# First-token products of the DeltaNet scans over 128 rows with zero tiles, in place of 16 rows

## Chip, cores, metric

One core of a Trainium2 chip. The metric is device microseconds (us) of one execution of the whole kernel. Before the change three runs gave 1980.45, 1980.38 and 1978.99 us, median 1980.38 us. The profiled execution took 1978.97 us, with a span from first to last instruction of 1977.2 us.

## The reference

One layer of a hybrid encoder over 1024 tokens, with 16 meta tokens put in front (1040 in all), 1024 channels, float32 throughout. What bears on the change is the gated DeltaNet branch, with 8 heads of 128 by 128 state, scanned forward and backward:

```python
h = rmsnorm(h_res, norm1_w)                       # h_res = [16 meta tokens, 1024 tokens]
q, k, v, z, b, a, ... = split(h @ w_in)           # q, k, v: 8 heads x 128
q, k, v = silu(depthwise_conv_centred([q, k, v])) # width 5
q, k = l2norm(q) * 128 ** -0.5, l2norm(k)
# for each head and direction, chunk by chunk:
#   L = strict_lower(beta * (k k^T) * decay);  solve (I + L) [u, w] = [beta v, beta e^g k]
#   v_new = u - w S;  o = (q e^g) S + (q k^T * decay) v_new
#   S     = S * e^g_last + (k e^(g_last - g))^T v_new
o = (o_fwd + o_bwd)[meta padding dropped];  o = rmsnorm(o) * silu(z)
```

After the scans come the short-convolution branch, gates, the output projection, and a SwiGLU block of 2816 hidden channels.

## The kernel before

The kernel has one long first phase (up to about 925 us) and then the projections and the SwiGLU block. In the first phase the input projection runs unit by unit: for each unit of 128 output channels, `dense_steps` (L328) multiplies the weights with the 1040 tokens, 24 products for each of two or three stretches of 320 to 512 tokens, each in split single-pass float32 halves. Names: `hTh` and `al` are the high and low parts of the input, `wh` and `wl` those of the weights, `pm` is the bank that they fill. Between these products a planner in the kernel places the rest: it keeps estimated clocks for TensorE, VectorE, ScalarE and GpSimd (`T`, advanced by the calls `pe(...)`, `V(...)`, `A(...)`), and resumes generators whose due time has come. Each generator issues a few instructions and yields the time at which its next step is due. So the order is fixed when the program is built, and instructions are issued on each engine in that order (`manual_schedule`).

Four generators work on a head in turn: `g_decay` (decays, into `PQ`), `g_norm` (norms of q and k, the products k k^T and k q^T), `g_inv` (inversion of I + L in 32-row blocks, partly over DRAM with small DMAs) and `g_scan` (the state recurrence). Chunks have 128 tokens here; chunk index 8 stands for the first 16 (meta) tokens, `META = 16`, whose slots are handled apart, with tiles of 16 rows:

- `g_norm`, L562 and L563: the first 16 tokens of `kT` (channels by tokens) are turned with a TensorE transpose (in the profile the helper's line, L98) into `pt[:16]`, and the 16x16 product k k^T is made. Then four transposes of the next chunks follow (`tok(0)`). L567 copies the turned tokens into `kn[:16, 8]`, L572 the product into `Nm`.
- `g_inv`, L696 to L698: the inverse of the 16x16 block comes back by DMA from DRAM into `Pm`, a tile of 16x16.
- `g_scan`, L788 to L796: transposes of `vT` in three groups of three, the first of which begins with the 16 tokens; L795 scales each into `vS`, on ScalarE.
- `g_scan`, L803: `Pm` times `vS[:16, 8]`, a product with 16 rows of contraction and 16 output rows; L806 (VectorE) scales the 16 rows into `w`; L808: `kn[:16, 8]` times `w[:16]`, 16 rows of contraction and 128 output rows, gives the state `S0` (L811) with which the forward scan starts. L853 to L899 are the scan's loop over chunks, all its products 128 by 128.

In the profile a float32 product that is not split takes two passes, so a product of this kind counts as two MATMULs, and a transpose as one. A MATMUL row reads, for example, `16*128 16x128`: 16 rows and 128 columns of the array in use, and a moving operand of 16 partitions by 128 elements.

Of the kernel before, what the change touches and what calls it, by code (L numbers as in the profile page):

```python
# [8 lines left out]
F32 = mybir.dt.float32  # L9
F32R = mybir.dt.float32r  # L10
I32 = mybir.dt.int32
AF = mybir.ActivationFunctionType
# [4 lines left out]
P = 128  # L17
# [3 lines left out]
META = 16  # L21
# [27 lines left out]
def encoder_layer(ctx: ExitStack, tc: tile.TileContext, x, meta, norm1_w, w_in, w_ba,  # L49
                  dn_conv_w, A_log, dt_bias, dn_norm_w, sc_conv_w, w_bdn, w_bsc,  # L50
                  w_out, norm2_w, w_gu, w_down, final_w, out):
    nc = tc.nc
# [12 lines left out]
    def uid(s):  # L65
        cnt["n"] += 1
        return f"{s}_{cnt['n']}"
# [7 lines left out]
    def psd():  # L75
        return ps.tile([P, 512], F32, tag="e", name=uid("pe"), bufs=3)

    def pss():
        return ps.tile([P, 512], F32, tag="d", name=uid("pd"), bufs=3)
# [15 lines left out]
    mm = nc.tensor.matmul  # L95

    def transpose(dst, src, n=P):
        nc.tensor.transpose(dst, src, ident[:n, :n])  # L98
# [18 lines left out]
    def wload(src, j):  # L117
        wh, wl, raw = staged([P, KT, P])
        nc.sync.dma_start(raw, src[j])
        split(wh, wl, raw)  # L120
        return wh, wl
# [136 lines left out]
    def pe(ns):  # L258
        T["pe"] += ns
        return T["pe"] + HOP  # L260

    def V(n, kind=0):
        return on("dve", (68 + 1.042 * n, 130 + 1.042 * n, 130 + 0.52 * n)[kind])

    def A(n):
        return on("act", 144 + 0.834 * n)
# [19 lines left out]
    def enqueue(lane, gen):  # L286
        j = Job(gen)
        if not lanes[lane]:
            spent[lane] = max(spent[lane], min(spent.values()))
        lanes[lane].append(j)  # L290
        return j
# [179 lines left out]
    def cs(c):  # L471
        return slice(META + c * P, META + (c + 1) * P)
# [32 lines left out]
    def norm_job(st_, ssk1, cc, ce, he, y, tmp, sk):  # L505
        nc.vector.tensor_tensor(out=ce, in0=cc, in1=he, op=ALU.mult)
        V(18)
        yield T["dve"] + DEP
        yield from rsqrt_steps(y, ssk1, tmp)
        nc.vector.tensor_tensor(out=sk, in0=y, in1=ssk1, op=ALU.mult)  # L510
        V(9)
# [25 lines left out]
    def g_norm(h, st_):  # L537

        kq = st_["kq"]
        kT, qT = kq[:, 0], kq[:, 1]  # L540
        small = dn.tile([P, 9, 12], F32, tag="small", name=uid("small"), bufs=3)
        st_["small"] = small
        ssk, ssq, rk2, ssk1, y, tmp, sk = (small[:, :, i] for i in range(7))
        cc, ce = small[:, :, 7:9], small[:, :, 9:11]
        nc.gpsimd.memset(small, 1.0)
        kn = dn.tile([P, 9, P], F32, tag="kn", name=uid("kn"), bufs=2)
        st_["kn"] = kn

        def square(src, dst, p=P):
            jk = dn.tile([P, P], F32, tag="jk", name=uid("jk"))  # L550
            nc.scalar.activation(jk[:p], src, AF.Square, accum_out=dst)
            return on("act", 400)
# [6 lines left out]
            return pt, pe(4 * 107)  # L559

        pt = psd()
        transpose(pt[:META, :P], kT[:, 0:META])  # L562
        mm(pt[:META, P:P + META], kT[:, 0:META], kT[:, 0:META], start=True, stop=True)  # L563
        t = pe(120)
        nxt = tok(0)
        yield t
        nc.scalar.copy(kn[:META, 8], pt[:META, :P])  # L567
        A(P)
        square(pt[:META, :P], ssk[:META, 8:9], META)
        Nm = dn.tile([META, META], F32, tag="Nm", name=uid("Nm"), bufs=2)  # L570
# [5 lines left out]
        for c2 in range(4):  # L576
            pt, t = nxt
# [5 lines left out]
            for c in range(2):  # L583
                for a, s in ((0, ssk), (1, ssq)):
                    t = square(pt[:, c, a], s[:, 2 * c2 + c:2 * c2 + c + 1])
# [31 lines left out]
        for c in range(NC):  # L617
# [3 lines left out]
            pk, t = nxt.pop(0)  # L621
# [15 lines left out]
                ask()  # L637
        enqueue("norm", norm_job(st_, ssk1, cc, ce, he, y, tmp, sk))

    def g_inv(h, st_):  # L640

        NP, Nm = st_["NP"], st_["Nm"]

        nd = dr.tile([4, NC, 2, 32, 32], F32, tag="nd", name=uid("nd"), bufs=2)
        ndm = dr.tile([META, META], F32, tag="ndm", name=uid("ndm"), bufs=2)
        fN = dn.tile([P, 32, 32], F32, tag="fN", name=uid("fN"))
# [42 lines left out]
        pdm = dr.tile([META, META], F32, tag="pdm", name=uid("pdm"), bufs=2)  # L691
        nc.sync.dma_start(pdm.unsqueeze(0), mP)
        yield T["dve"] + LAND
        for b in range(4):
            nc.sync.dma_start(NP[B(b), :, :, B(b)].rearrange("j c d i -> j (c d) i"), pd[b].rearrange("c d j i -> j (c d) i"))
        Pm = dn.tile([META, META], F32, tag="Pm", name=uid("Pm"), bufs=2)  # L696
        st_["Pm"] = Pm
        nc.sync.dma_start(Pm, pdm)  # L698

        Xe = dn.tile([P, NC, 32], F32, tag="Xe", name=uid("Xe"))  # L700
        XT = dn.tile([P, 2, 512], F32, tag="XT", name=uid("XT"))
# [21 lines left out]
        pt = pss()[:, :256].rearrange("p (c i) -> p c i", c=NC)  # L723
# [31 lines left out]
        pt = pss().rearrange("p (c i) -> p c i", c=NC)  # L755
# [16 lines left out]
    def g_scan(h, st_):  # L772
        nonlocal freed
        kq, vT, small, kn, NP, PQ, Pm = (st_[k] for k in ("kq", "vT", "small", "kn", "NP", "PQ", "Pm"))
        kT, qT = kq[:, 0], kq[:, 1]
        ssk, ssq, rk2, ssk1, y, tmp, sk = (small[:, :, i] for i in range(7))
        cc, ce = small[:, :, 7:9], small[:, :, 9:11]
        sso = small[:, :, 11]
        vS = dn.tile([P, 9, P], F32, tag="vS", name=uid("vS"))
        yield from take("scan")  # L780

        def newbank():
            return pss().rearrange("p (a n) -> p a n", a=4)

        for grp in ((8, 0, 7), (1, 2, 3), (4, 5, 6)):
            pt = newbank()
            for i, c in enumerate(grp):
                if c == 8:  # L788
                    transpose(pt[:META, i], vT[:, 0:META])
                else:  # L790
                    transpose(pt[:, i], vT[:, cs(c)])
            yield pe(330)
            for i, c in enumerate(grp):
                p = META if c == 8 else P
                nc.scalar.activation(vS[:p, c], pt[:p, i], AF.Copy, scale=sk[:p, c:c + 1])  # L795
                A(P)  # L796
        yield T["act"] + HOP

# [1 line left out]


        bank = newbank()
        mm(bank[:META, 0], Pm, vS[:META, 8], start=True, stop=True)  # L803
        yield pe(215)
        w = dn.tile([P, P], F32, tag="w0", name=uid("w"))
        nc.vector.tensor_scalar(out=w[:META], in0=bank[:META, 0], scalar1=ce[:META, 8, 0:1], scalar2=None, op0=ALU.mult)  # L806
        yield V(P, 1)
        mm(bank[:, 1], kn[:META, 8], w[:META], start=True, stop=True)  # L808
        yield pe(215)
        S0 = dn.tile([P, P], F32, tag="S0", name=uid("S"), bufs=2)  # L810
        nc.vector.tensor_copy(S0, bank[:, 1])  # L811
# [35 lines left out]
        for i in range(NC):  # L847
# [6 lines left out]
            t = pe(215 * len(act_))  # L854
# [5 lines left out]
            for d in act_:  # L860
                c = cd[d]
# [3 lines left out]
                t = V(P, 1)  # L865
# [5 lines left out]
            w = [None, None]  # L871
            v2 = [None, None]
            for d in range(2):
                c = cd[d]
                w[d] = dn.tile([P, P], F32, tag=f"w{d}", name=uid("w"))
                nc.scalar.activation(w[d], b2[:, 2 + d], AF.Copy, scale=ce[:, c, d:d + 1])  # L876
                t = A(P)
            for d in range(2):
                c = cd[d]
# [3 lines left out]
            if i < NC - 1:  # L883
# [3 lines left out]
                t = pe(430)  # L887
# [4 lines left out]
            if i < NC - 1:  # L892
                yield t
                for d in range(2):
# [6 lines left out]
                    t = V(P, 1)  # L901
# [30 lines left out]
        for c4 in range(2):  # L932
            oT = vS[:, 4 * c4:4 * c4 + 4]
            pt = newbank()
# [48 lines left out]
    def start_streams():  # L983
        nonlocal ndec, nnorm, ninv, nscan
        h = ndec
        if h < H and h < freed + 2 and not decs:
            decs.append([g_decay(h, heads[h]), T["dve"] + HOP, h])
            ndec += 1
        h = nnorm
        if h < H and h < ndec and h < freed + 2 and not norms and all(k in heads[h] and heads[h][k]() for k in ("tk", "tq")):  # L990
            norms.append([g_norm(h, heads[h]), T["dve"] + HOP, h])
            nnorm += 1
        h = ninv
        if h < H and not invs and heads[h].get("normed"):
            invs.append([g_inv(h, heads[h]), T["dve"] + HOP, h])
            ninv += 1
        h = nscan
        if h < H and not scans and heads[h].get("inverted") and "tv" in heads[h] and heads[h]["tv"]():
            scans.append([g_scan(h, heads[h]), T["dve"] + HOP, h])
            nscan += 1  # L1000
# [22 lines left out]
    with tc.tile_pool(name="st", bufs=1) as st:  # L1023
# [37 lines left out]
        scale = {}  # L1061
# [306 lines left out]
    dn = ph1.enter_context(tc.tile_pool(name="dn", bufs=1))  # L1368
# [299 lines left out]
    for j in range(KT):  # L1668
        w = wload(w_bsc, j)
# [12 lines left out]
    for j in range(KT):  # L1682
        w = wload(w_bdn, j)
# [114 lines left out]
    t = KT - 1  # L1798
# [40 lines left out]
    AA, bank, bank2, po2 = [A0, A1, None, None], [pss()], [None] * 4, [psd()]  # L1839
# [304 lines left out]
```

## Time and profile before

| what | value |
|---|---|
| three runs | 1980.45, 1980.38, 1978.99 us; median 1980.38 us |
| profiled execution | 1978.97 us |
| its span | 1977.2 us, granted TensorE clock 0.999 |
| VectorE busy | 1395.8 us (71%), 3017 instructions |
| ScalarE busy | 838.5 us (42%) |
| GpSimd busy | 106.6 us (5%) |
| DMA | 251.52 MB, mean 127 GB/s |

PE is TensorE, PEld its weight loads, DVE is VectorE, ACT ScalarE, POOL GpSimd, SP the engine that issues most DMAs. Starts in the timeline are counted from the span's start. The end of a MATMUL is modelled, so this document reads TensorE's pace from the starts of successive MATMULs: what a group of instructions costs is the distance between starts around it, less the usual distance of the projection's products beside it.

### The profile page before, as it was taken

What the parts mean: (1) busy time and instruction counts of PE and PEld (TensorE: products, weight loads), DVE (VectorE), ACT (ScalarE), POOL (GpSimd) and SP (SyncE); (2) the same over time, 40 slices, a digit from 0 to 9 for tenths busy, and PEclk for the clock granted to TensorE, in tenths of its full rate; (3) what the DMA queues carried; (4) which work ended last, traced back from release to release, by engine and by line L of the source; (5) the groups of instructions that cost most, each with busy time, mean ns of one, the idle gap of its engine ahead of it and who ended that gap; (6) DMA issues with size and microseconds to landing.
All of it is one profiled execution on the core that took longest, in us unless ns stands there. A gap on an engine that the chain in (4) does not pass through costs nothing.

```text
span 1977.2 us, 31834 instructions
## 1 busy us (share of the span) xinstructions
PE 1961.2 (99%) x11992; PEld 1715.3 (87%) x11992; DVE 1395.8 (71%) x3017; ACT 838.5 (42%) x1968; POOL 106.6 (5%) x407
## 2 busy tenths in 40 slices
PE   9999999999999999999999999999999999999998
PEld 8999999999999999888888888888888888888887
DVE  7888688888888888844954544469676766746575
ACT  6472354636464646344444221225333333334344
POOL 2011101010101010100000000000000000000000
PEclk9999999999999999999999999999999999999999
DMA  4122122222222212222236752123366654477654
GB/s 145 59 88 81 55 87 60 76 60 76 60 76 60 76 60 76 70 87 90 102 128 229 252 167 97 65 86 111 124 220 243 253 183 165 170 278 243 193 176 165
DMA packets 124703, 251.52 MB, mean 127 GB/s; under 512 B 44988, under 2 KB 46453, under 8 KB 122117
## 3 DMA queue, kind: packets, MB, share of 16 engines
q1 hardware_dynamic: 123957, 248.44, 37.7%
q8 instruction: 94, 1.54, 0.3%
q10 hardware_dynamic: 592, 1.05, 0.1%
q14 instruction: 60, 0.49, 0.1%
HBM read 181.20 MB, written 68.25 MB: 126 GB/s over the span
## 4 chain that ended last, share of the span: by engine, by line
PE 92%; DVE 3%; DMA 2%; ACT 1%; issue 1%; SPq 0%; POOL 0%; DVEq 0%; POOLq 0%; ACTq 0%
PE pm L328 30%; PE pd L1441 14%; PE pe L1441 7%; PE pm L1441 5%; PE pe L136 2%; PE pe L135 2%; PE pe L134 2%; PE pd L869 1%; PE pd L890 1%; PE pd L853 1%; PE pe L2051 1%; PE pe L2052 1%; PE pe L2050 1%; PE pd L856 1%; PE pe L590 1%; PE pd L886 1%
## 5 line engine op out<-in xcount | busy, mean ns | idle before, releaser
L328 PE MATMUL pm<-hTh,wh 128*128 128x320 f32 (+4 forms) x1248 | 428.3, 348 | 0.3 <-ACT hTh L1091 0.2
L328 PE MATMUL pm<-al,wh 128*128 128x320 f32 (+4 forms) x1248 | 427.4, 348 | 0.0
L328 PE MATMUL pm<-hTh,wl 128*128 128x320 f32 (+4 forms) x1248 | 425.8, 346 | 0.1
L328 PEld LDWEIGHTS pm<-hTh,wh 128*128 128x128 f32 x1248 | 233.8, 188 | 12.8 <-issue 2.1
L328 PEld LDWEIGHTS pm<-hTh,wl 128*128 128x128 f32 x1248 | 233.9, 188 | 10.6 <-issue 0.4
L328 PEld LDWEIGHTS pm<-al,wh 128*128 128x128 f32 x1248 | 233.9, 188 | 9.7
L102 DVE TENSOR_TENSOR al<-raw,ring_h 128x1024 fp32r<-128x1024 f32 x73 | 88.6, 1222 | 64.7 <-ACT ring_h L101 63.9
L101 ACT CAST ring_h<-raw 128x1024 fp32r<-128x1024 f32 x73 | 76.6, 1053 | 106.2 <-PE pe L2052 35.0
L350 DVE SCALAR_TENSOR_TENSOR kq<-ra,wc,kq 128x520 f32<-128x520 f32 x128 | 96.5, 754 | 4.7 <-ACT kq L380 3.4
L977 DVE TENSOR_TENSOR wl<-raw,wh 128x512 fp32r<-128x512 f32 x112 | 75.8, 687 | 31.4 <-ACT wh L980 30.9
L876 ACT ACTIVATE w<-pd,small 128x128 f32<-128x128 f32 x128 | 39.8, 363 | 125.2 <-PE pd L869 124.6
L483 DVE TENSOR_TENSOR tm<-fP,fN 128x135 f32<-128x135 f32 (+23 forms) x248 | 71.6, 289 | 5.4 <-POOL mP L682 1.0
L487 DVE TENSOR_TENSOR fP<-fP,tm 128x135 f32<-128x135 f32 (+23 forms) x248 | 71.4, 288 | 5.1
L980 ACT CAST wh<-raw 128x512 fp32r<-128x512 f32 x112 | 66.3, 621 | 3.7 <-issue 3.6
L101 ACT CAST wh<-raw 128x1024 fp32r<-128x1024 f32 x37 | 38.8, 1048 | 46.6 <-PE pm L135 14.8
L1989 ACT ACTIVATE b<-b 128x512 f32<-128x512 f32 x20 | 12.6, 631 | 104.5 <-DVE b L1407 104.5
L843 ACT ACTIVATE jk<-NP 128x128 f32<-128x128 f32 x64 | 19.9, 311 | 76.5 <-DVE NP L839 75.4
L1441 PE MATMUL pd<-b_hl,wh 128*128 128x512 f32 x168 | 51.9, 390 | 0.0
L899 DVE SCALAR_TENSOR_TENSOR S<-S,eGl,pd 128x128 f32<-128x128 f32 x104 | 31.5, 340 | 28.0 <-PE pd L886 27.9
L863 DVE SCALAR_TENSOR_TENSOR r<-pd,negEG,vS 128x128 f32<-128x128 f32 x120 | 36.7, 344 | 20.4 <-PE pd L853 20.2
L1407 DVE TENSOR_TENSOR b<-pd,b 128x512 f32<-128x512 f32 x21 | 14.5, 689 | 51.8 <-PE pd L1441 51.8
L102 DVE TENSOR_TENSOR wl<-raw,wh 128x1024 fp32r<-128x1024 f32 x37 | 45.1, 1218 | 7.4 <-ACT wh L101 7.3
(629 smaller groups left out, 4783.0 us busy)
## 6 DMA issues: line engine op xcount, KB each, us to landing
raw<-in_w_in_dram SPq DMA_DIRECT2D x72, 512.0 KB
raw<-in_w_gate_up_dram SPq DMA_DIRECT2D x44, 512.0 KB
sums<-in_w_down_dram SPq DMA_DIRECT2D x22, 512.0 KB
t_d<-sums SPq DMA_DIRECT2D x11, 1024.0 KB
raw<-s_d SPq DMA_DIRECT2D x44, 256.0 KB
raw<-t_d SPq DMA_DIRECT2D x44, 256.0 KB
act_d<-b SPq DMA_DIRECT2D x43, 256.0 KB
raw<-act_d SPq DMA_DIRECT2D x33, 256.0 KB
```

The costliest lines, as they stand in the source:

```text
L101: nc.scalar.copy(hi, src)
L102: nc.vector.tensor_tensor(out=lo, in0=src, in1=hi.bitcast(F32), op=ALU.subtract)
L134: mm(po[:m, :n], wh[:, k, :m], xhk[:, t0:t0 + n], start=(k == 0), stop=False)
L135: mm(po[:m, :n], wh[:, k, :m], xlk[:, t0:t0 + n], start=False, stop=False)
L328: mm(po[:, :n], ww[:, k], f(k)[:, t0:t0 + n], start=i == 0, stop=i == 3 * KT - 1)
L350: nc.vector.scalar_tensor_tensor(out=acc, in0=raw[:, h0 + t:h0 + t + hn], scalar=wc[:, t, col:col + 1], in1=acc, op0=ALU.mult, op1=ALU.add)
L483: nc.vector.tensor_tensor(out=tv, in0=fP[:, 0:r, j:j + 1].broadcast_to([P, r, n]), in1=fN[:, j:j + 1, j + 1:32].broadcast_to([P, r, n]), o ...
L487: nc.vector.tensor_tensor(out=fP[:, 0:r, j + 1:32], in0=fP[:, 0:r, j + 1:32], in1=tv, op=ALU.subtract)
L876: nc.scalar.activation(w[d], b2[:, 2 + d], AF.Copy, scale=ce[:, c, d:d + 1])
L977: nc.vector.tensor_tensor(out=u[1][1][:, k], in0=u[2][:, k], in1=u[1][0][:, k].bitcast(F32), op=ALU.subtract)
L980: nc.scalar.copy(u[1][0][:, k], u[2][:, k])
L1441: mm(po, x[:, k], at(y, k), start=i == 0 and not add_to, stop=i == 11, skip_group_check=add_to)
```

## The change

All products and copies of the first 16 tokens are made over 128 rows and columns. In `g_norm` the first 128 tokens of `kT` are turned, and their whole 128x128 product is made; of it the 16x16 corner is used as before. `kn[:, 8]` gets 128 rows, of which 16 matter. Three tiles of 128x128, `wide`, are made once and set to zero on GpSimd in `g_inv` of the first head. Two of them take the place of `Pm`, for even and odd heads: the DMA fills the 16x16 corner alone. The third takes the place of `w`: VectorE writes its first 16 rows. In `g_scan` the first 128 tokens of `vT` are turned and scaled, and the two products (L803 and L808 before, L801 and L806 after) contract over 128 rows; zeros stand against whatever is in rows 16 to 127.

```diff
         pt = psd()
-        transpose(pt[:META, :P], kT[:, 0:META])
-        mm(pt[:META, P:P + META], kT[:, 0:META], kT[:, 0:META], start=True, stop=True)
+        transpose(pt[:, :P], kT[:, 0:P])
+        mm(pt[:, P:2 * P], kT[:, 0:P], kT[:, 0:P], start=True, stop=True)
...
-        nc.scalar.copy(kn[:META, 8], pt[:META, :P])
+        nc.scalar.copy(kn[:, 8], pt[:, :P])
...
-        Pm = dn.tile([META, META], F32, tag="Pm", name=uid("Pm"), bufs=2)
-        st_["Pm"] = Pm
-        nc.sync.dma_start(Pm, pdm)
+        if not wide:
+            wide.extend(dn.tile([P, P], F32, tag=f"wide{i}", name=uid("wide")) for i in range(3))
+            for t in wide:
+                nc.gpsimd.memset(t, 0.0)
+        Pm = st_["Pm"] = wide[h % 2]
+        nc.sync.dma_start(Pm[:META, :META], pdm)
...
-                if c == 8:
-                    transpose(pt[:META, i], vT[:, 0:META])
-                else:
-                    transpose(pt[:, i], vT[:, cs(c)])
+                transpose(pt[:, i], vT[:, 0:P] if c == 8 else vT[:, cs(c)])
             yield pe(330)
             for i, c in enumerate(grp):
-                p = META if c == 8 else P
-                nc.scalar.activation(vS[:p, c], pt[:p, i], AF.Copy, scale=sk[:p, c:c + 1])
+                nc.scalar.activation(vS[:, c], pt[:, i], AF.Copy, scale=sk[:, c:c + 1])
...
-        mm(bank[:META, 0], Pm, vS[:META, 8], start=True, stop=True)
+        mm(bank[:, 0], Pm, vS[:, 8], start=True, stop=True)
         yield pe(215)
-        w = dn.tile([P, P], F32, tag="w0", name=uid("w"))
+        w = wide[2]
         nc.vector.tensor_scalar(out=w[:META], in0=bank[:META, 0], scalar1=ce[:META, 8, 0:1], scalar2=None, op0=ALU.mult)
         yield V(P, 1)
-        mm(bank[:, 1], kn[:META, 8], w[:META], start=True, stop=True)
+        mm(bank[:, 1], kn[:, 8], w, start=True, stop=True)
```

The planner's estimates are the same numbers in both kernels, and so is the order on every engine, but for three instructions on POOL. TensorE around the first head's two products, with the size of the result at a row's end (L803 has 16 rows of it), before:

```order
L328 MATMUL pm<-hTh,wh 128x384
L328 MATMUL pm<-al,wh 128x384
L803 MATMUL pd<-vS,Pm 16x128
L328 MATMUL pm<-hTh,wl 128x384
L328 MATMUL pm<-hTh,wh 128x384
L328 MATMUL pm<-al,wh 128x384
L328 MATMUL pm<-hTh,wl 128x384
L328 MATMUL pm<-hTh,wh 128x384
L328 MATMUL pm<-al,wh 128x384
L808 MATMUL pd<-w,kn 128x128
L328 MATMUL pm<-hTh,wl 128x384
```

and after, where the same two products are L801 and L806:

```order
L328 MATMUL pm<-hTh,wh 128x384
L328 MATMUL pm<-al,wh 128x384
L801 MATMUL pd<-vS,wide 128x128
L328 MATMUL pm<-hTh,wl 128x384
L328 MATMUL pm<-hTh,wh 128x384
L328 MATMUL pm<-al,wh 128x384
L328 MATMUL pm<-hTh,wl 128x384
L328 MATMUL pm<-hTh,wh 128x384
L328 MATMUL pm<-al,wh 128x384
L806 MATMUL pd<-wide,kn 128x128
L328 MATMUL pm<-hTh,wl 128x384
```

Nothing moved; the six projection products between the two stay six. POOL in the first head's `g_inv`, after (`mP` is the 16x16 inverse, `ra` a row buffer of the convolutions, `XT` a tile of the inversion):

```order
L681 TENSOR_TENSOR mP<-mP,tm 1x15
L417 MEMSET ra 128x2
L698 MEMSET wide 128x128
L698 MEMSET wide 128x128
L698 MEMSET wide 128x128
L705 MEMSET XT 32x8x32
L706 MEMSET XT 32x8x32
L417 MEMSET ra 128x2
```

The three rows on `wide` are new, between `ra` and `XT`; the first head's DMA into `wide` waits for POOL, where that into `Pm` did not. The later heads' DMAs wait for what they waited for.

More of the change, by code (lines that the diff above doesn't have):

```diff
@@ L638, in g_norm @@
         enqueue("norm", norm_job(st_, ssk1, cc, ce, he, y, tmp, sk))
+    wide = []
     def g_inv(h, st_):
```

## The prediction

> **What bounds the kernel now.** I read the page first: how busy each engine is, and who stands on the chain of waits that ended last.
>
> ```profile
> PE 1961.2 (99%) x11992; PEld 1715.3 (87%) x11992; DVE 1395.8 (71%) x3017; ACT 838.5 (42%) x1968; POOL 106.6 (5%) x407
> PE 92%; DVE 3%; DMA 2%; ACT 1%; issue 1%; SPq 0%; POOL 0%; DVEq 0%; POOLq 0%; ACTq 0%
> ```
>
> TensorE is busy 99% of the span and holds 92% of the chain. So time that TensorE loses inside its own stream is time of the kernel, unless it falls where the chain lies on another engine. A busy share of 99% does not say that no pace is lost, since ends of MATMULs are modelled. So next I read the timeline of TensorE around the instructions that the change touches, by starts. The first head, around L803 and L808 (start, length, instruction; L328 is the projection):
>
> ```profile
> 214.40 0.34 PE L328 MATMUL pm<-al,wh 128*128 128x384 f32 x1
> 214.67 0.39 PE L803 MATMUL pd<-vS,Pm 16*16 16x128 f32 x2
> ...
> 215.27 0.34 PE L328 MATMUL pm<-hTh,wh 128*128 128x384 f32 x1
> 215.44 0.34 PE L328 MATMUL pm<-al,wh 128*128 128x384 f32 x1
> 215.62 0.33 PE L328 MATMUL pm<-hTh,wl 128*128 128x384 f32 x1
> ...
> 215.97 0.34 PE L328 MATMUL pm<-al,wh 128*128 128x384 f32 x1
> 216.23 0.48 PE L808 MATMUL pd<-w,kn 16*128 16x128 f32 x2
> ...
> 216.93 0.34 PE L328 MATMUL pm<-hTh,wh 128*128 128x384 f32 x1
> ```
>
> Undisturbed, an L328 product of 384 elements starts 0.17 to 0.18 us after the last one (215.27, 215.44, 215.62); call it 0.174. From 214.40 to 215.27 two such products and the two passes of L803 fit in: 0.87 - 2 x 0.174 = **0.52 us** for L803. From 215.97 to 216.93 the same way: 0.96 - 0.35 = **0.61 us** for L808. The last head, beside products of 512 elements:
>
> ```profile
> 875.94 0.40 PE L328 MATMUL pm<-hTh,wl 128*128 128x512 f32 x1
> ...
> 876.92 0.39 PE L328 MATMUL pm<-al,wh 128*128 128x512 f32 x1
> 877.15 0.39 PE L328 MATMUL pm<-hTh,wl 128*128 128x512 f32 x1
> 877.38 0.40 PE L328 MATMUL pm<-hTh,wh 128*128 128x512 f32 x1
> ...
> 878.46 0.40 PE L328 MATMUL pm<-hTh,wl 128*128 128x512 f32 x1
> ```
>
> Here the distance is 0.23; L803 costs 0.98 - 0.46 = 0.52 and L808 1.08 - 0.46 = 0.62. These are the first and the last of 8 heads. What do whole 128x128 products cost in the same place? The first head's next block, two products of two passes each:
>
> ```profile
> 217.62 0.34 PE L328 MATMUL pm<-al,wh 128*128 128x384 f32 x1
> 217.80 0.38 PE L853 MATMUL pd<-S,kq 128*128 128x128 f32 x2
> 218.02 0.39 PE L856 MATMUL pd<-S,kq 128*128 128x128 f32 x2
> ...
> 218.42 0.33 PE L328 MATMUL pm<-hTh,wh 128*128 128x384 f32 x1
> ```
>
> 0.80 - 0.35 = 0.45 us, so **0.226 us** for one product, 0.113 a pass. A product with an eighth of the rows costs more than twice as much as a whole one, on both sides of it: L803 starts 0.27 after the product before it instead of 0.17, and the product after it loses about as much. L853 has a semaphore to wait for as well and loses nothing, so I put the loss down to the change of shape in the array.
>
> [...]
>
> **The change part by part.** L803 becomes a whole product: 0.52 - 0.226 = 0.294 us, by 8 heads **2.35 us** gained. L808: 0.615 - 0.226 = 0.39, by 8 heads **3.1 us**. Next the first 16 tokens in `g_norm`, first and last head:
>
> ```profile
> 99.08 0.34 PE L328 MATMUL pm<-al,wh 128*128 128x384 f32 x1
> 99.26 0.27 PE L98 MATMUL pe<-ident,kq 128*16 128x128 f32 x1
> 99.46 0.21 PE L563 MATMUL pe<-kq 128*16 128x16 f32 x2
> ...
> 100.28 0.33 PE L328 MATMUL pm<-hTh,wh 128*128 128x384 f32 x1
> ```
>
> ```profile
> 764.75 0.34 PE L328 MATMUL pm<-al,wh 128*128 128x384 f32 x1
> ...
> 765.94 0.31 PE L328 MATMUL pm<-hTh,wh 128*128 128x322 f32 x1
> ```
>
> One narrow transpose, two narrow passes and four whole transposes cost 1.20 - 0.35 = 0.85, and 1.19 - 0.35 = 0.84. Afterwards they are seven whole passes, at 0.113 each 0.79. That gains 0.06 a head. The narrow passes lose their gap but get longer, and the two nearly cancel. Of the 8 places two, at 262.9 and 372.4 us, fall in stretches where the chain is not on TensorE (below) and count nothing: 6 x 0.06 = **0.36 us**. Bounds: nothing, if a pass costs 0.01 more than those of L853, and 0.28 a head, 1.7 us, if the two passes of the product hid wholly beside five transposes (0.57). The transposes of `vT`, one narrow and two whole:
>
> ```profile
> 301.16 0.34 PE L328 MATMUL pm<-hTh,wh 128*128 128x384 f32 x1
> 301.34 0.49 PE L98 MATMUL pd<-ident,vT 128*16 128x128 f32 x3
> ...
> 301.84 0.34 PE L328 MATMUL pm<-hTh,wl 128*128 128x384 f32 x1
> ```
>
> 0.68 - 0.35 = 0.33 for three, 0.11 each. They run at a whole pass's price already, and nothing is gained or lost: **0**.
>
> Off TensorE: ScalarE's copies (L567, L795) keep their elements per row, with more rows. GpSimd gets three fills, and the first head's DMA waits for them:
>
> ```profile
> L1246 POOL MEMSET Eb<- 128x128 f32 x1 | 0.2, 205 | 0.0
> 162.24 0.10 POOL L417 MEMSET ra<- 128x2 f32 x1 [6.43 <-DVE small L495]
> 194.91 0.48 SPq L698 DMA_DIRECT2D Pm<-pdm x1
> ```
>
> A fill of this size took 205 ns, three take 0.6 us. They stand ahead of 6.43 us in which POOL idled, over 30 us before the DMA is issued. So they cost **0**. Without that cover it would be 0.6 us, once.
>
> One wait remains for L803: the last of ScalarE's copies into `vS`.
>
> ```profile
> PEld pd L803 <- ACT vS L795: 2.2, 6, 0.4
> ```
>
> Its weight load idled 2.2 us in 6 heads, and the wait's last signal was ScalarE's. I take most of that as the gap itself, because L803 costs the same 0.52 in the first and in the last head while the copies end at other distances. But where the gap goes, ScalarE may be late by a part of it. Bounds are 0 and the whole of L803's gain, 2.35; I take 0.2 us, nearer to 0 since the gap after L803 cannot come from a wait before it.
>
> Sum: 2.35 + 3.1 + 0.36 - 0.2 = **5.6 us**. The profiled execution took 1978.97 us, and 1978.97 - 5.6 = 1973.4. It is at the low end of what was shown: with it and the three runs the mean is 1979.7. So I predict 1979.7 - 5.6 = **1974.1 us**, 0.28% faster.
>
> **The rivals.** First, the gain is made but waits take it back. The chain leaves TensorE for long in three places; entry and return of the first two, and the end of the third:
>
> ```profile
> 258.25 0.46 PE pd L853 x4
> 295.56 0.67 PE pe L590 x2
> 334.87 0.46 PE pd L869 x4
> 390.71 0.42 PE pd L736 x7
> 695.09 0.61 ACT XT L760
> ```
>
> All sixteen products L803 and L808 lie outside these stretches. If the other engines entered each stretch no earlier than now, TensorE would only wait longer, and what was gained before 695 us would be lost: heads 0 to 4, with L803 and L808 of heads 5 to 7 left, 3 x 0.68 + 0.1, **2.2 us**, hence 1977.5. For it speaks that DVE has little idle time there, a fifth in the row below. Against it: each stretch starts from a TensorE instruction, which moves earlier, and DVE has slack to follow.
>
> ```profile
> 218.00:258.70 40.70, 40.70 (x279) 38.64 (x278) 32.24 (x105) 14.42 (x49) 8.50 (x33) 1.00 0.14 42
> ```
>
> From the first head's L808 to the first stretch DVE was busy 32.24 of 40.70 us (the third number pair); 8.5 us of slack stands against 0.7 to make up.
>
> Second, on the other side: the gaps are no matter of shape, and stay. Then only the added work shows.
>
> ```profile
> L803 PEld LDWEIGHTS pd<-vS,Pm x16: 87/89/92, 214.7 to 876.3; 16*16 16x16 f32 x16
> L853 PEld LDWEIGHTS pd<-S,kq x240: 186/189/193, 217.6 to 919.0; 128*128 128x128 f32 x120
> ```
>
> A weight load of 16 columns took 89 ns, one of 128 columns 189: 0.1 us more for each of 16 passes of L803 and 16 of L563, 3.2 us. L563's 16 passes also stream 128 elements in place of 16, at most a whole pass's 0.113 each, 1.8 us. It decides if the loads cannot slip under the products before them while the gaps stay: **5.0 us slower**, 1984.7. Against it: whole products of L853 in the same stream hide all but 0.113 a pass.
>
> [...]
>
> Third, the change does only half of what it says: the gap before a product goes but the one after stays, as when it comes from the unsplit two-pass form. Then half, 2.8 us, 1976.9. Against it: L853 has two passes of this form, with no gap on either side.
>
> **How the numbers follow.** Forecast 0.78; waits take the gain back 0.10; half 0.06; gaps stay 0.04; anything else, such as TensorE's own pauses falling elsewhere, 0.02 on the slow side. The forecast's own bounds: 4.3 us of gain, with nothing from `g_norm` and half of L803's lost to its wait, to 7.1, with 1.7 from `g_norm` and no wait. With the runs' spread of 0.7 us to either side that is 1971.9 to 1976.1. The range reaches to the first rival: 1972.0 to 1977.5. A difference of 0.2%, 4 us, is about what a measurement of this kernel can tell from none. So faster 0.78, same 0.16, slower 0.06.
>
> **What would show it.** In the changed profile, starts around L801 and L806 should leave 0.23 us each; if 0.5 stays, the shape was not the reason. The `g_norm` block should cost 0.79, the `vT` group 0.33. The three stretches off TensorE should be as long as now, each entered earlier by what was gained before it; if they end at the same times, the first rival holds. Weight loads of L801 should not idle for `vS`. The part after 925 us should keep its length. The prediction is wrong if TensorE's waits for DVE and ACT grow by over 2 us in the first phase.

## The result, and the profile after

| what | before | after |
|---|---|---|
| median (14 runs each, same chip) | 1979.68 us (1978.12 to 1981.19) | 1975.4 us (1972.61 to 1978.34) |
| profiled execution, its span | 1978.97, 1977.2 us | 1978.34, 1976.6 us |

The ratio is 0.9979, interval 0.9971 to 0.9987: the change makes the kernel 4.3 us faster. Two repeats (below) gave 0.9973 and 0.9976. The profiled execution of after is the longest of its 14 runs, so its span hides most of the gain. The page of after, busy times and chain:

```profile
PE 1958.5 (99%) x11992; PEld 1721.5 (87%) x11992; DVE 1396.1 (71%) x3017; ACT 838.7 (42%) x1968; POOL 107.9 (5%) x410
PE 90%; DVE 4%; DMA 3%; ACT 1%; issue 1%; SPq 0%; DVEq 0%; ACTq 0%
```

TensorE has as many instructions as before and is 2.7 us less busy. That is all these two lines can say; the places of the change say more. TensorE's timeline of after around the first head's two products (start, length, instruction):

```profile
215.56 0.34 PE L328 MATMUL pm<-al,wh 128*128 128x384 f32 x1
215.74 0.38 PE L801 MATMUL pd<-vS,wide 128*128 128x128 f32 x2
215.88 0.42 PE L328 MATMUL pm<-hTh,wl 128*128 128x384 f32 x1
216.14 0.34 PE L328 MATMUL pm<-hTh,wh 128*128 128x384 f32 x1
...
216.83 0.34 PE L328 MATMUL pm<-al,wh 128*128 128x384 f32 x1
217.01 0.38 PE L806 MATMUL pd<-wide,kn 128*128 128x128 f32 x2
217.15 0.42 PE L328 MATMUL pm<-hTh,wl 128*128 128x384 f32 x1
217.41 0.33 PE L328 MATMUL pm<-hTh,wh 128*128 128x384 f32 x1
```

Read as in the prediction: L801 costs 216.14 - 215.56 - 0.35 = **0.23 us** (0.52 before), L806 217.41 - 216.83 - 0.35 = **0.23** (0.61). L801 starts 0.18 after the product ahead of it, the projection's own distance: the gap is gone on both sides. Over all 8 heads L801 costs 0.224 to 0.230 and L806 0.225 to 0.235. The `g_norm` block of the first head:

```profile
100.43 0.34 PE L328 MATMUL pm<-al,wh 128*128 128x384 f32 x1
100.61 0.27 PE L98 MATMUL pe<-ident,kq 128*128 128x128 f32 x1
100.71 0.39 PE L563 MATMUL pe<-kq 128*128 128x128 f32 x2
100.94 0.60 PE L98 MATMUL pe<-ident,kq 128*128 128x128 f32 x4
...
101.55 0.34 PE L328 MATMUL pm<-hTh,wh 128*128 128x384 f32 x1
```

1.12 - 0.35 = 0.77 us (0.85 before); 0.770 to 0.789 over the heads. The `vT` group stays at 0.33. By places a head gains 0.295 + 0.387 + 0.070 = 0.752 us on average, eight heads 6.02.

What hides it in this one execution? The stretches table shows two windows of 4 us (columns: stretch, length, busy time of PE, PEld, DVE, ACT, POOL, granted clock, DMA share, GB/s), first of after:

```profile
11.00:15.00 4.00, 3.43 (x17) 3.09 (x18) 3.54 (x9) 1.58 (x4) 1.40 (x2) 0.61 1.03 411
288.00:292.00 4.00, 3.76 (x103) 2.96 (x104) 3.90 (x12) 1.42 (x5) 0.00 (x0) 0.57 0.02 5
```

and of before:

```profile
11.00:15.00 4.00, 3.60 (x23) 2.69 (x24) 3.89 (x11) 2.82 (x6) 1.66 (x3) 1.00 1.03 411
288.00:292.00 4.00, 4.00 (x114) 3.59 (x113) 3.87 (x11) 0.89 (x3) 0.00 (x0) 1.00 0.02 4
```

The clock granted inside such a window is 0.50 (290 to 291 us of after). So 0.57 over 4 us is 0.43 x 4 / 0.5 = 3.4 us at half clock; an estimate from that is at most about 1.7 us lost where TensorE sets the pace. There are two such windows in after's trace, and none in before's until the last few us of the run. Is this of the change, or of the execution? That was the first thing to settle.

### The profile page after: what moved, and what is told of

Its sections match the earlier page's. It is cut to its first block, busy times and chain, and to the rows that moved or that the text cites. A ratio compares the mean times of both kernels' runs of the same rounds, so it can differ in the third digit from the quotient of the medians.

```text
span 1976.6 us, 31840 instructions
## 1 busy us (share of the span) xinstructions
PE 1958.5 (99%) x11992; PEld 1721.5 (87%) x11992; DVE 1396.1 (71%) x3017; ACT 838.7 (42%) x1968; POOL 107.9 (5%) x410
## 4 chain that ended last, share of the span: by engine, by line
PE 90%; DVE 4%; DMA 3%; ACT 1%; issue 1%; SPq 0%; DVEq 0%; ACTq 0%
PE pm L328 30%; PE pd L1439 12%; PE pe L1439 6%; PE pm L1439 4%; PE pe L135 2%; PE pe L136 2%; PE pe L134 2%; PE pe L590 1%; PE pd L867 1%; PE pd L888 1%; PE pd L851 1%; PE pe L2049 1%; PE pe L2048 1%; PE pe L2050 1%; DMA sums<-in_w_down_dram 1%; PE pd L854 1%
## 5 line engine op out<-in xcount | busy, mean ns | idle before, releaser
L1439 PE MATMUL pd<-b_hl,wh 128*128 128x512 f32 x168 | 51.9, 390 | 0.0
```

What stands on the lines that cost most here:

```text
L1439: mm(po, x[:, k], at(y, k), start=i == 0 and not add_to, stop=i == 11, skip_group_check=add_to)
```

## The experiments

Two readings stood against each other. By the first (S in the expectations) the gap belongs to the shape of the product in the array, the gain by places is real, and half-clock windows fall by chance. By the second (R) the changed kernel loses part of the gain in the stretches at 258 to 296 and 335 to 391 us in every run, which is the prediction's first rival.

**The changed kernel again**, unchanged, twice.

> The changed kernel once more, for a second trace. Theory S (the shape of the products costs the gaps): L801 and L806 again 0.22 to 0.24 us each in all 8 heads, and the median 3.5 to 5 us under the kernel before. Theory K (what the first trace of the changed kernel lost beside that, +1.4 us before 17 us and about +0.9 us around 290 us, are two windows of 3.41 us in which the clock was granted at half, which come and go from run to run): here such windows lie elsewhere or are missing, the mean granted clock goes with the run's time, and a run without the two windows has a span of 1973 to 1974 us. Rival R (the stretches where the chain is off TensorE take the gain back in every run): the losses at 288 to 296 us and at 385 to 391 us (0.45 us) come again at the same places with the same sizes, whatever the clock.

> The changed kernel a third time, for comparison on the same chip: 1974.5 to 1975.5 us, the first part ending at 926 to 927.5 us where no half-clock window falls in it and 1.7 us later for each that does; the last part anywhere from 1045 to 1047.5 us. Theory S by sums: without windows the first part ends 5.5 to 6 us before that of the kernel before (932.2 us in both its traces).

Measured: 1974.97 us (8 runs) against 1979.83, ratio 0.9973 (0.9963 to 0.9984); and 1975.39 us (11 runs) against 1980.29, ratio 0.9976 (0.9967 to 0.9985). Neither trace has a half-clock window before the end. The stretches table of the second repeat:

```profile
288.00:292.00 4.00, 4.00 (x58) 3.80 (x45) 3.44 (x10) 0.72 (x2) 0.00 (x0) 1.00 0.00 0
```

So R, as a loss in every run, falls. Are the windows of the change all the same? In the thirteen traces, each one with a half-clock window before the last few us has a mean granted clock of 0.997 or 0.998, each one without 0.999. Over all runs with a recorded clock, 8 of 33 of the changed kernel and 11 of 56 of the kernel before stand at 0.998: the windows are about as frequent in both. The place near 288 us came again in two more traces of kernels with wide products, the ladder and the 80 columns below, shown in this order, and in none of those with 16-row products; these are too few to tell whether the change makes that one place likelier.

```profile
289.00:293.00 4.00, 4.00 (x50) 3.62 (x37) 3.44 (x10) 0.73 (x2) 0.00 (x0) 0.57 0.00 0
289.00:293.00 4.00, 4.00 (x74) 3.64 (x63) 3.47 (x10) 0.72 (x2) 0.00 (x0) 0.59 0.01 4
```

The chain's rows of the second repeat for the first stretch off TensorE, entry and return:

```profile
257.07 0.46 PE pd L851 x4
294.39 0.67 PE pe L590 x2
```

37.32 us, where before had 295.56 - 258.25 = 37.31: the stretch keeps its length and starts earlier.

**The kernel before again**, as the partner of these traces.

> The kernel before once more, for a second trace. Theory N (the first trace of the kernel before had a short last part by chance: 1045.1 us from the last projection product to the end, against 1045.9 to 1048.2 in five traces of other kernels): the last part takes 1046 to 1048 us here, with TensorE waiting 0.5 to 2 us each near 1470, 1510 or 1567 us for VectorE behind the w_down sums, and the first part ends at 932 us. Rival B (the earlier end of the first part causes those waits): the last part takes 1045.1 us again, within 0.3.

Measured: 1979.88 us. The first phase's end, as the start of the last projection product, in this kernel:

```profile
932.23 0.39 PE L328 MATMUL pm<-hTh,wl 128*128 128x512 f32 x1
```

and in the second repeat of the changed one:

```profile
927.09 0.39 PE L328 MATMUL pm<-hTh,wl 128*128 128x512 f32 x1
```

The first phase is 5.14 us shorter; between the first trace of before and the first repeat it is 932.20 - 927.36 = 4.84. The rest took 1045.91 us here (span 1978.1), between what the two theories expected of it, and 1045.39 in the changed kernel (1972.5). Over all thirteen traces of this study the rest took 1045.05 to 1048.99 us with no order by kernel; so a single pair of times can be off by some us for reasons that this change doesn't touch.

**A ladder of shapes**, a different one in each head of the changed kernel. The products leave rows or columns out.

> The changed kernel with another shape in each head. The second product (L806 of the changed kernel) contracts over 16, 32, 48, 64, 65, 80, 96, 112 rows in heads 0 to 7; the first (L801) has 16 rows and 16 columns, then 128 rows with 16, 32, 64, 96 columns, then 16, 64, 96 rows with 128 columns; the k k^T product of the first tokens has 16, 32, 48, 64, 80, 96, 112, 128 columns and 16 moving elements. [...] Up to 64 rows or columns about 0.6 us for the second product and 0.5 to 0.6 for the first; from 65 rows or columns on 0.23, as for 128. Rival S2 (cost follows the number of idle rows): it falls gradually from 0.61 at 16 rows to 0.23 at 112. Rival W (the wait for other engines costs the gap): 0.5 to 0.6 in all heads, whatever the shape.

```diff
+        ca = (16, 32, 48, 64, 80, 96, 112, 128)[h]
-        mm(pt[:, P:2 * P], kT[:, 0:P], kT[:, 0:P], ...)
+        mm(pt[:ca, P:P + META], kT[:, 0:ca], kT[:, 0:META], ...)
...
+        r1, c1_ = ((16, 16), (128, 16), (128, 32), (128, 64), (128, 96), (16, 128), (64, 128), (96, 128))[h]
-        mm(bank[:, 0], Pm, vS[:, 8], ...)
+        mm(bank[:c1_, 0], Pm[:r1, :c1_], vS[:r1, 8], ...)
...
+        r2 = (16, 32, 48, 64, 65, 80, 96, 112)[h]
-        mm(bank[:, 1], kn[:, 8], w, ...)
+        mm(bank[:, 1], kn[:r2, 8], w[:r2], ...)
```

The second product (L809 here) with 64 rows, in the fourth head, and with 65, in the fifth:

```profile
510.77 0.40 PE L328 MATMUL pm<-hTh,wh 128*128 128x512 f32 x1
511.10 0.48 PE L809 MATMUL pd<-wide,kn 64*128 64x128 f32 x2
511.51 0.50 PE L328 MATMUL pm<-al,wh 128*128 128x512 f32 x1
511.85 0.39 PE L328 MATMUL pm<-hTh,wl 128*128 128x512 f32 x1
...
607.85 0.39 PE L328 MATMUL pm<-hTh,wh 128*128 128x512 f32 x1
608.08 0.39 PE L809 MATMUL pd<-wide,kn 65*128 65x128 f32 x2
608.22 0.48 PE L328 MATMUL pm<-al,wh 128*128 128x512 f32 x1
608.54 0.39 PE L328 MATMUL pm<-hTh,wl 128*128 128x512 f32 x1
```

1.08 - 0.46 = 0.62 us and 0.69 - 0.46 = 0.23. All rungs, worked out this way from starts and distances in nanoseconds:

| product | us |
|---|---|
| second, 16, 32, 48, 64 rows | 0.617, 0.619, 0.623, 0.626 |
| second, 65, 80, 96, 112 rows | 0.239, 0.242, 0.239, 0.228 |
| first, 16 rows x 16 columns; 16, 64, 96 rows x 128 | 0.518; 0.613, 0.630, 0.239 |
| first, 128 rows x 16, 32, 64, 96 columns | 0.526, 0.537, 0.577, 0.225 |
| `g_norm` block, 16, 32, 48, 64 columns | 0.842, 0.880, 0.888, 0.919 |
| `g_norm` block, 80, 96, 112, 128 columns | 0.680, 0.699, 0.709, 0.729 |

The price doesn't follow the number of rows: it steps between 64 and 65 rows, and between 64 and 80 columns. The product reads the same tiles in all heads, and so waits for the same engines. The expectation had put the step at 64; that was a supposition, and what in the array sets the step no run shows.

**A small product that need not wait**: 16 rows, its operand long ready, between the two products of the changed kernel, once in even heads and twice in a row in odd ones. Nothing uses its result.

> The changed kernel with a product of 16 rows added in each head between the two products, from operands that have long been there, so that it waits for nobody; even heads make it once, odd heads twice in a row; its result is used by nothing. Theory S (shape): it costs about 0.6 us once, though it waits for nobody, and twice in a row 0.6 plus one product, 0.8 us, since the shape changes only at the two ends. Rival W (the wait): 0.23 and 0.45 us.

```diff
+        for _ in range(1 + h % 2):
+            mm(bank[:, 2], kn[:META, 8], kn[:META, 8], start=True, stop=True)
+            pe(215)
+        yield T["pe"] + 400
```

TensorE's timeline, first head (once), and second head (twice, merged into one row):

```profile
217.32 0.34 PE L328 MATMUL pm<-al,wh 128*128 128x384 f32 x1
217.59 0.48 PE L807 MATMUL pd<-kn 16*128 16x128 f32 x2
218.00 0.44 PE L328 MATMUL pm<-hTh,wl 128*128 128x384 f32 x1
218.28 0.34 PE L328 MATMUL pm<-hTh,wh 128*128 128x384 f32 x1
```

```profile
309.32 0.39 PE L328 MATMUL pm<-hTh,wl 128*128 128x512 f32 x1
309.64 0.71 PE L807 MATMUL pd<-kn 16*128 16x128 f32 x4
310.27 0.50 PE L328 MATMUL pm<-hTh,wh 128*128 128x512 f32 x1
310.61 0.40 PE L328 MATMUL pm<-al,wh 128*128 128x512 f32 x1
```

0.96 - 0.35 = 0.61 us for one, 1.29 - 0.46 = 0.83 for two. Over the heads one small product costs 0.61 to 0.62 us and two cost 0.83 to 0.85. The load still names one semaphore of VectorE; in the heads at 217.6 and 805.0 us the profile shows no signal of it in the idle time ahead of the load, so nothing was left to wait for, and the cost is the same there, 0.615 and 0.619. The gap is there without a wait, and the second small product adds 0.22, a whole product's price. So the gap is paid at the two ends of a group, not by each product. With the ladder, that excludes a wait as the cause and puts the price on the change of shape; what the array does in that time no trace shows.

**Only the `g_norm` and `vT` parts** of the change, with the two products, and the tiles `Pm` and `w` that they read, as before.

> The kernel before with the parts in g_norm and the transposes of v alone over 128 rows; the two products at the scan's start stay at 16 rows. Theory S: the block in g_norm goes from 0.845 to 0.77 us, the group of v transposes stays at 0.33, L803 and L808 stay at 0.52 and 0.61: 0.5 us gained, 1979.2, no difference that can be measured. Rival R (the gain comes from wider transposes and copies, not from the two products): 3 to 4 us gained here.

The two products, against the changed kernel:

```diff
-        mm(bank[:, 0], Pm, vS[:, 8], start=True, stop=True)
+        mm(bank[:META, 0], Pm, vS[:META, 8], start=True, stop=True)
-        mm(bank[:, 1], kn[:, 8], w, start=True, stop=True)
+        mm(bank[:, 1], kn[:META, 8], w[:META], start=True, stop=True)
```

Measured: 1980.27 us (11 runs) against 1979.83, ratio 1.0002 (0.9993 to 1.0011). No gain can be told from none here, and in the trace the two products cost 0.52 and 0.61 us again; they carry most of the change's gain.

**80 columns in place of 128** in the `g_norm` product, 16 moving.

> The changed kernel, but the k k^T product of the first tokens takes 80 columns of the array and 16 moving elements in place of 128 and 128. Theory S: 80 columns are past the step, so the block costs what 80 columns cost in the run with a shape for each head, 0.68 us, against 0.77 in the changed kernel and 0.845 before: 0.7 us more gained over 8 heads, some 0.03%, less than the times can tell. Rival L (a pass costs a whole weight load whatever the shape): 0.77 as with 128 columns.

```diff
-        mm(pt[:, P:2 * P], kT[:, 0:P], kT[:, 0:P], start=True, stop=True)
+        mm(pt[:80, P:P + META], kT[:, 0:80], kT[:, 0:META], start=True, stop=True)
```

TensorE's timeline of the block:

```profile
100.13 0.34 PE L328 MATMUL pm<-al,wh 128*128 128x384 f32 x1
...
100.41 0.25 PE L563 MATMUL pe<-kq 128*80 128x16 f32 x2
...
101.16 0.33 PE L328 MATMUL pm<-hTh,wh 128*128 128x384 f32 x1
```

1.03 - 0.35 = 0.68 us, 0.680 to 0.687 in all heads, where the changed kernel has 0.77 and before 0.85. A product can be short and clear of the step. Eight times 0.09 is 0.7 us, too little for the medians: 1975.12 us (8 runs) against 1980.59, ratio 0.9973 (0.9962 to 0.9983).

**The sums of the SwiGLU block later.** After's trace shows TensorE waiting for VectorE at L1439, 1.8 us in 2 places, where before's list of waits shows no such row. I took it for the order of VectorE's sums of `w_down` and made them one round later.

> The changed kernel; in the SwiGLU block the four subtractions on the w_down rows and the write of their result are made one round later than the load, in place of right behind it. Theory N: in the last part TensorE's waits near 1470, 1510 and 1567 us go, since VectorE no longer stands waiting for that load ahead of what TensorE needs; the last part takes 1044.5 to 1045 us, 1 to 2 us less than in the changed kernel, 1973 us. Rival D (the DMA queue itself is the limit there): the waits move to other lines of the same stretch and the time stays within 0.5 us.

```diff
-        for o_, a, b in (...): sub(o_, a, b)
-        nc.sync.dma_start(t_d[k], r)
+        def combine():
+            for o_, a, b in (...): sub(o_, a, b)
+            nc.sync.dma_start(t_d[k], r)
+        return combine
...
+        if late: late(); late = None
...
-            down_sums(j - 4, sg)
+            late = down_sums(j - 4, sg)
```

A miss: 1976.55 us (10 runs) against 1980.59, ratio 0.9978 (0.9969 to 0.9988). The waits near 1470 and 1510 us went, and one came elsewhere in TensorE's timeline:

```profile
1526.10 4.43 PE L1439 MATMUL pd<-b,u_hl 128*128 128x512 f32 x12 [2.65 <-DVE b L1405]
```

The stretches table of this run shows why the row is so long: a half-clock window falls into it, and its 12 products take 4.43 us where the 12 near 1510 us take 3.02 in after.

```profile
1525.50:1529.50 4.00, 3.40 (x9) 2.73 (x10) 2.43 (x4) 0.63 (x1) 0.00 (x0) 0.57 0.54 221
```

The last part took 1048.99 us, the longest of all; about 1.4 us of it is that window, so this one trace says little of the edit. What paces that stretch stays open.

**The pause at 286 us.** L590 makes the products k k^T and k q^T; in the third head TensorE waits there for VectorE's last use of a bank. TensorE's waits, first repeat of the changed kernel:

```profile
PE pe L590 <- DVE PQ L629: 1.8, 2, 1.4
```

The next kernels let the planner ask for that head's products 1.9 us later, in the changed kernel, with the 80 columns, and in the kernel before.

```diff
-            freed_at.append(V(2 * P) + 100)
+            freed_at.append(V(2 * P) + (2000 if h == 2 else 100))
```

> The changed kernel; for the third head the planner takes a bank of the products k k^T, k q^T as free 1.9 us later than it did, so that TensorE gets projection products where it waited 1.7 us for VectorE (286 to 288 us). The order after that place differs in many small ways. Theory K: with no pause there no half-clock window of 3.41 us falls at 288 to 292 us in any trace, and fewer runs have a mean granted clock of 0.998 (7 of 22 runs of the changed kernel had it); the median falls by 0.5 to 2 us. Rival: the pause moves to another place of the third head, the share of such runs stays, and the time stays or grows by up to 2 us.

> The changed kernel with both: the k k^T product of the first tokens at 80 columns and 16 moving elements, and the third head's bank taken as free 1.9 us later. If the two add up (0.7 us from the product, 1 us from the pause), the median is 1.5 to 2 us under the changed kernel's of the same call, 1973.3 us, with the first part ending at 924 to 924.5 us. Rival: the later bank was a lucky sample of five runs; then the time is within 1 us of the changed kernel.

> The kernel before, with 16-row products, and only the third head's bank taken as free 1.9 us later. If the pause costs by itself, it gains here what it gains in the changed kernel, 1 to 1.5 us: 1978.5 us. If the pause only takes back what the wider products gain (rival R, the first rival of the prediction), nothing is gained here: 1979.7, within 0.5.

| kernel | median us | before, beside it | ratio |
|---|---|---|---|
| changed, later | 1973.93 (5 runs) | 1980.59 | 0.9963 (0.9949 to 0.9976) |
| changed, 80 columns, later | 1972.52 (5 runs) | 1980.29 | 0.9964 (0.9951 to 0.9976) |
| before, later | 1979.01 (11 runs) | 1980.29 | 0.9993 (0.9984 to 1.0002) |

The wait at L590 is gone from the list of all three; one of 0.8 us for VectorE, ahead of the 64x64 products of an inversion, is new in it. The last projection product starts at 924.99 us in the changed kernel and, with 80 columns, at 924.34, where the changed kernel alone had 927.09, but eight transposes that stood ahead of it now come behind it. The first product of the next phase at L136 has the same work ahead of it in all of them: it starts at 926.38 and 925.72 us, against 927.78, so 1.4 and 2.1 us are gained. With 80 columns it is the best version that ran, 2.9 us under the median of the changed kernel measured beside it (1975.39 us), though their intervals of the ratio overlap. In the kernel before, the same edit's 1.3 us can't be told from none by the medians. Its trace speaks for a gain: from the first projection product to that L136 it takes 917.04 us, where the kernel before took 918.97 and 919.08; in the changed kernel the same edit makes 914.08 into 912.53. So this looks like an improvement of its own that the change doesn't need, on one trace of each.

## Why the prediction came out as it did

Right in direction, mechanism and size: 1974.1 predicted, 1975.4 measured, inside the range. The number is helped by luck: the places gained more than the 5.6 us of the sum, 6.02, and a loss that the sum does not have took back about 1 us. By its steps:

- *The gap is of the shape.* Shown, by the ladder's step and by the small product without a wait. The second rival (gaps stay, longer loads) and the third (half of the gap goes) fall with it (what stays open is why transposes with 16 columns are exempt, see the last section): the gap went on both sides, although the weight load doubled, from 89 ns for L803 in before to 188 for L801, in the profile's group of that line in after:

```profile
L801 PEld LDWEIGHTS pd<-vS,wide x16: 187/188/188, 215.6 to 874.3; 128*128 128x128 f32 x16
```

- *L803 2.35 us, L808 3.1 us.* 0.295 x 8 = 2.36 and 0.387 x 8 = 3.10.
- *`g_norm` 0.36 us.* The block gained 0.070, not 0.06, in all 8 heads: 0.56 by places. Leaving out the place in the first stretch was right: between the same two projection products around that stretch (257.63 and 298.27 us in before) the two traces of before took 40.65 and 40.67 us, the two repeats 40.69 and 40.66. For the place in the second stretch nothing can be told: there the same kernel differs by 0.5 us from trace to trace (58.06 and 58.54 before, 57.89 and 58.27 in the repeats).
- *0.2 us for the wait of L801.* Nothing: the group of L801 shows no idle time ahead of its loads. The 2.2 us that the profile of before put down to ScalarE's `vS` was the gap itself. `vT` and the fills cost 0, as said.
- *The sum, 5.6 us.* By places 6.02. In the first phase 4.84 and 5.14 arrived in the two pairs of traces, so some 0.9 to 1.2 us is given back, most of it at places that I did not name. The step that fell short is that only the three long stretches were examined as places where waits could take the gain back. Of those the first took no more than its own 0.07, the second can't be told, and 0.1 went right behind the third (6.92 and 6.94 us before, 7.03 and 7.01 in the repeats, from 690.24 us of before). The inversions of heads 7 and 8 took 0.6 to 1.0 in the four pairings of these traces. Between the same two projection products, head 8 (863.04 to 870.18 us in before) took 7.14, 6.86 and 7.33 us in the three traces with 16-row products, and 7.32 to 7.75 in the five of the changed kernel, the 80 columns and the later sums (7.13 in the ladder): a tendency, whose ranges touch. For head 7 (783.08 to 790.07) it is 6.98 to 7.00 in the three, and 6.98, 7.00, 7.16, 7.20 and 7.48 in the five (6.98 in the ladder): a loss of some executions, not of each. TensorE's waits for VectorE and ScalarE, the prediction's sign of being wrong, did not grow in the first phase: the list of waits adds up to 5.1 and 4.7 us before, and 4.1 and 4.4 in the repeats.

One of these places, around the 64x64 products of the last inversion, in before (L757, L758):

```profile
867.50 0.39 PE L328 MATMUL pm<-hTh,wl 128*128 128x512 f32 x1
867.82 0.27 PE L757 MATMUL pd<-XT,NP 64*64 64x64 f32 x1
867.83 0.27 PE L758 MATMUL pd<-XT,NP 64*64 64x64 f32 x1
...
868.90 0.50 PE L328 MATMUL pm<-hTh,wh 128*128 128x512 f32 x1
```

and in the first repeat of the changed kernel (L759, L760), with ScalarE's copy that L760 reads:

```profile
862.96 0.39 PE L328 MATMUL pm<-hTh,wl 128*128 128x512 f32 x1
863.17 0.36 ACT L752 COPY XT<-pd 32x256 f32<-32x256 f32 x1 [0.94 <-DVE XT L751]
863.29 0.31 PE L759 MATMUL pd<-XT,NP 64*64 64x64 f32 x2
863.68 0.24 PE L760 MATMUL pd<-XT,NP 64*64 64x64 f32 x1
...
864.73 0.50 PE L328 MATMUL pm<-hTh,wh 128*128 128x512 f32 x1
```

From product to product 1.40 us became 1.77. L760 starts 0.15 us after ScalarE's copy ends (863.17 + 0.36 = 863.53), so it looks held by that copy. The copy is late because the step before it is: a pause of 0.6 us on TensorE, which waits for nothing that the profile shows, fell ahead of the last L738 there, whose result ScalarE waits for, and ahead of the last L739 in before, which it doesn't wait for. This is read from one pair of traces, and was not tried. Another such pause stands in the second repeat of the changed kernel, in the inversion of head 7:

```profile
783.54 0.41 PE L328 MATMUL pm<-hTh,wh 128*128 128x320 f32 x1 [0.22 <-issue]
```

- *The part after 925 us keeps its length.* Only in the sense that the kernel doesn't change it: 1045.05 to 1048.99 us from trace to trace, more than the whole difference between forecast and result. The profiled execution of before lay at the low end of its runs, that of after at the high end.

Why the medians show 4.3 to 4.9 us and the first phase 4.84 to 5.14 was not settled. The two ranges overlap. Half-clock windows (0.8 us and more each, below) and the length of the last part make larger differences than that between single executions.

## What to carry to other kernels

A small float32 product among whole 128x128 ones need not be cheap because it is small (here 0.61 us with 16 rows, 0.23 with 128): look at the distance of starts on both sides of it, and if it costs more than a whole product, bring it over 64 rows and columns with zeros (here the second product cost 0.626 us with 64 rows and 0.239 with 65, the `g_norm` block 0.919 with 64 columns and 0.680 with 80) or group the small ones, so that the two ends are paid once (here 0.61 to 0.62 us for one, 0.83 to 0.85 for two in a row). Price a saving on a busy engine by starts in its stream, then look for every place downstream where the engine arrives at another one's heels; not only the longest. One profiled execution can hide a gain of 0.2% (the two spans here differ by 0.6 us, the medians by 4.3): compare pieces of the span between traces before explaining a total.

## What the runs showed of the hardware that was not expected

- The price of a product of another shape is a step: 0.62 us for 16 to 64 rows and 0.23 to 0.24 for 65 to 112. Transposes with 16 columns (`128*16`) do not pay the gap: three cost 0.33 us with one narrow among them, and 0.33 with none, where a product with 16 columns cost 0.53. Why they are exempt no run here shows.
- TensorE drops to half clock for 3.4 us in some executions: before the last few us once or twice in six of the thirteen traces, near 10 to 12 us, near 288 to 290, and once at 1525.7, and not at all in the other seven. One near 288 us makes the stretch around it 0.8 to 1.2 us longer (41.51 us in after, 41.84 in the ladder and with 80 columns, against 40.65 to 40.69). It follows a pause of 1.3 to 1.5 us at L590, but the repeats have the same pause, and before one of 1.3, at a clock of 1.00. So the same pause has a half-clock window behind it in one run and none in another; what sets the windows off no run here shows.
